# Outputs of the grouped attention kept in a tile on chip, and two sets of evacuations moved to the pool of eight small buffers

## The chip, the core and the metric

The kernel runs on one core of a Trainium2 chip. The metric is the device time of one execution in microseconds, as the median of several runs. Engines are named as the profile names them: PE is TensorE (PEld its weight loads), DVE is VectorE, ACT is ScalarE, POOL is GpSimd, SP is SyncE, which here only issues DMAs.

## What is computed

Two layers of an encoder trunk over 1024 tokens of width 1024 and a memory of 256 tokens. Each layer mixes tokens with four head groups side by side, attends to the memory, and ends in a gated ConvFFN. Cut to the part that the change touches:

```python
for l in range(DEPTH):                        # DEPTH = 2
    h = rms_norm(x, norm_mix[l])
    (ml_q, ml_k, ml_v, ml_o, ml_g, pool_u,
     d_q, d_k, d_v, g_q, g_k, g_v) = jnp.split(h @ w_in[l], splits, axis=-1)
    y_a = mlstm_mixer(ml_q, ml_k, ml_v, ml_o, ml_g, ...)       # 4 heads of 64, chunks of 64
    y_b = pool_mixer(pool_u, pool_w[l], pool_scale[l])
    y_c = diff_attention(d_q, d_k, d_v, ...)                   # 4 heads, two softmaxes each
    y_d = gqa_axial(g_q, g_k, g_v, ...)                        # 4 query heads, 2 key heads
    x = x + jnp.concatenate([y_a, y_b, y_c, y_d], axis=-1) @ w_out[l]
    x = x + cross_attention(rms_norm(x, norm_cross[l]), rms_norm(mem, norm_mem[l]), ...)
    x = x + conv_ffn(rms_norm(x, norm_ffn[l]), ...)
```

Inside the cross attention, the keys and values of the memory are `kv = memn @ w_ckv`, and the keys are normed per head.

## The kernel before

Activations lie transposed, features on the partitions: eight tiles of 128 features by 1024 tokens. Every factor of a product is split into a high and a low part (`hi`, `lo`), and a product is three matmuls (L353 hi·hi, L355 lo·hi, L357 hi·lo) that add up in one PSUM bank.

**Buffers.** All tiles come from pools with a fixed number of buffers; a tile that is asked for waits until the oldest holder of a buffer has been read for the last time, by a DMA too. `h` has 16 tiles of 128x1024, `t` 17 and `z` 4 of that size, `s` has eight tiles of 128x512, `e` two of 128x512. PSUM has two score tiles `sc`, three banks `tp` (of which one carries the attention's P·V sums) and one bank `fl` for filler work. `raw` and `wp` hold weights as they arrive and as they were split.

**Order.** A scheduler that models the engines puts the instructions of each engine in an order by priority. The steps of the attention (`attend`, L553) run under a raised priority. Between them the kernel pumps *filler*: generators in three queues that make a few matmuls at a time. Filler of queue 0 runs in the order in which it was filed: `memory_keys` (L1296), `memory_values` (L1367), the load and the split of the mixer's outputs (`mixed`, L1184, through `load_pair`, L1251), and the output projection (`residual_steps`, L1261).

**The mixer** (`mix`, L1069) of a layer first makes the projections. `ml_project` (L781) makes the mLSTM's query, key, value gate tiles; each of its two halves is scaled by DVE (L790) into an `e` tile and stored to DRAM (for the key `mkd`, L795). Then come the grouped attention and the differential attention. Both go in *passes*: one pass makes the scores of 128 queries against 1024 keys (L685, L688 grouped; L634 differential), DVE takes the row maximum (L479), ACT makes the exponentials (L482, an `h` tile). Then, four times 128x512, PE transposes probabilities (L537), ACT copies them as the high part into an `s` tile (L541), DVE makes the low part in another (L542), and PE makes the product with the values (L527, L528, L530). The grouped attention has 32 passes a layer, the differential one 64, whose two softmaxes POOL combines (L510, L511). For each pair of softmaxes DVE makes the factors of the combination (L508, L509).

**Outputs of the grouped attention.** `gqa_head` (L672) adds the two halves of a block of 64 features by 256 queries into half of an `s` tile and, for each second block, stores 64x512 to DRAM (`yd`). The filler `mixed` loads features 6 and 7 from there into a `z` tile and splits it into two `t` tiles (L1257, L1258). The other features of `yd` come from the mLSTM and from pooling.

**The memory's pairs.** `memory_keys` norms the keys and writes them as pairs in `e` tiles (L1361 ACT, L1362 DVE), stored to `ckd`. `memory_values` makes the products of the values, 24 matmuls a block (L1382 to L1384) in the `fl` bank, evacuates each as a pair into an `e` tile (L1388 ACT, L1389 DVE) and stores it to `cvd`.

**The output projection** is filler too: per 128 output features, four chunks of 18 matmuls (six feature tiles, three products each; 128x256) into halves of the `fl` bank, each evacuated by DVE onto the residual in a `z` tile (L1278). The last of eight feature tiles goes through a `tp` bank.

Of the kernel before, what the change touches and what calls it, by code (L numbers as in the profile page):

```python
# [23 lines left out]
HF = 512  # L24
# [27 lines left out]
class Net:  # L52
# [616 lines left out]
        )  # L669
        return q  # L670

    def gqa_head(self, l, h, kh, kl, V, q, ahead):  # L672
        nc = self.nc
        f, hh = divmod(h, 2)
        out = []

        def group(g):
            ws, tasks = [], {}
            for i in range(2):
                q0 = (g * 2 + i) * P  # L680

                def scores(sc, q0=q0):
                    for n in range(2):
                        sl = slice(n * HF, (n + 1) * HF)
                        nc.tensor.matmul(sc[:, sl], lhsT=q[:, q0 : q0 + P], rhs=kh[:, sl], start=True, stop=False)  # L685
                    for n in range(2):
                        sl = slice(n * HF, (n + 1) * HF)
                        nc.tensor.matmul(sc[:, sl], lhsT=q[:, q0 : q0 + P], rhs=kl[:, sl], start=False, stop=True)  # L688

                tasks[2 * i] = self.softmax(scores, ws)  # L690

            def evac(a, b):
                if g % 2 == 0:
                    out.append(self.s_())
                o = out[-1][:64]
                nc.vector.tensor_tensor(out=o[:, g % 2 * 256 : g % 2 * 256 + 256], in0=a, in1=b, op=ALU.add)
                if g % 2:
                    nc.sync.dma_start(
                        out=self.YD[6 + f, hh * 64 : hh * 64 + 64, g // 2 * HF : (g // 2 + 1) * HF], in_=o
                    )  # L700

            return tasks, self.mix_values(ws, V, evac)

        for g in range(4):
            if g == 2:
                ahead()
            yield group(g)
# [73 lines left out]
    def ml_project(self, l, j, H, dst, scale=None, sigmoid=False):  # L781
# [1 line left out]
        w = self.weights(self.d["w_fm"][l, j])  # L783

        def evac(sl, ps):
            t = self.e_()
            if scale is None:
                nc.vector.tensor_tensor(out=t, in0=ps, in1=self.RB[:, sl], op=ALU.mult)
            else:
                nc.vector.scalar_tensor_tensor(  # L790
                    out=t, in0=ps, scalar=scale, in1=self.RB[:, sl], op0=ALU.mult, op1=ALU.mult
                )
            if sigmoid:
                nc.scalar.activation(t, t, AF.Sigmoid)
            (nc.scalar if sigmoid else nc.sync).dma_start(out=dst[:, sl], in_=t)  # L795
# [273 lines left out]
    def mix(self, l, H, st):  # L1069
# [109 lines left out]
        self.flush(2)  # L1179
        self.fill(self.memory_keys(l, mem, self.h_, nc.gpsimd))  # L1180

        Y, Y2 = [], []

        def mixed(ks):  # L1184
            for k in ks:
                Y.append(self.load_pair(self.YD[k], self.tr_, nc.gpsimd if k < 7 else None))
                yield 0

        def heads():
            nonlocal nxt  # L1190
            for h in range(4):
                now = nxt

                def ahead():
# [4 lines left out]
                    else:  # L1199
                        nxt = self.diff_keys(l, 0, self.h_), self.diff_query(l, 0, 0, self.h_)  # L1200

                for g, (tasks, mix) in enumerate(self.gqa_head(l, h, *now, ahead)):
                    if (h, g) == (3,0):
                        self.flush(1)
                        self.fill(mixed((0, 1, 2, 3)))
# [45 lines left out]
    def load_pair(self, src, alloc, lo_engine=None, stage=False):  # L1251

        nc = self.nc
        x = self.tile(self.pw, [P, S], F32, "raw", bufs=4) if stage else self.z_()
        nc.sync.dma_start(out=x, in_=src)
        hi, lo = alloc(F32R), alloc(F32R)
        nc.scalar.copy(hi, x)  # L1257
        (lo_engine or nc.vector).tensor_tensor(out=lo, in0=x, in1=hi.bitcast(F32), op=ALU.subtract)  # L1258
# [37 lines left out]
    def memory_keys(self, l, mem, alloc, lo_engine):  # L1296
# [54 lines left out]
        for h in range(4):  # L1351
# [5 lines left out]
                    out=x0(h, f), in0=x0(h, f), scalar=self.col(l, C_CK + f), in1=pb, op0=ALU.mult, op1=ALU.mult  # L1357
                )
            for f in range(2):
                pr = self.e_(F32R).rearrange("p (s n) -> p s n", n=MEM)  # L1360
                nc.scalar.copy(pr[:, 0], x0(h, f))  # L1361
                nc.vector.tensor_tensor(out=pr[:, 1], in0=x0(h, f), in1=pr[:, 0].bitcast(F32), op=ALU.subtract)  # L1362
                nc.sync.dma_start(out=self.CK[h, :, f], in_=pr.bitcast(F32))
# [3 lines left out]
    def memory_values(self, l, mem, lo_engine):  # L1367
        nc, d = self.nc, self.d
        H, r = mem
        for h in range(4):  # L1370
# [6 lines left out]
            for t in range(2):  # L1377
# [6 lines left out]
                    nc.tensor.matmul(ps, lhsT=xl[:, tok], rhs=wh, start=False, stop=k == KT - 1)  # L1384
                    yield 3 * MEM / 2400
                rt = r[:, t : t + 1]
                pr = self.e_(F32R).rearrange("p (s n) -> p s n", n=MEM)
                nc.scalar.activation(pr[:, 0], ps, AF.Identity, bias=0.0, scale=rt)  # L1388
                nc.vector.scalar_tensor_tensor(  # L1389
                    out=pr[:, 1], in0=ps, scalar=rt, in1=pr[:, 0].bitcast(F32), op0=ALU.mult, op1=ALU.subtract  # L1390
# [580 lines left out]
```

## Time and profile before

| | us |
|---|---|
| Median of three runs | 3478.75 (3475.57 to 3484.61) |
| The profiled execution | 3481.47 |
| Its span in the trace | 3479.7 |
| Busy: PE, DVE, ACT, POOL | 3302.7, 2091.0, 1438.3, 570.1 |
| Layer 0: grouped attention, about | 388 to 551 |
| Layer 0: differential attention, about | 551 to 736 |
| Layer 0: its drain and the end of the output projection | 736 to 767 |
| Layer 1: grouped attention, about | 2104 to 2276 |

The span is the time between the first and the last instruction in the trace of one execution. Busy time of PE is that of matmuls; its weight loads run beside them. The stages are read from the first and the last score pass of each attention, and from the last matmul of the output projection.

### The profile page before, as it was taken

The page shows a single profiled execution, that of the slowest core. Times are in us where ns is not written, and L with a number is a line of the kernel's source. Part 1 is how long each engine was busy: PE and PEld are TensorE (multiplying, and loading weights), DVE is VectorE, ACT ScalarE, POOL GpSimd, SP SyncE. Part 2 cuts the span into 40 slices and gives each one's busy share as a digit, 9 for nine tenths or more (in the row PEclk, how much of TensorE's full clock was granted, in tenths as well). Part 3 has the DMA queues.
Part 4 walks back from the last instruction along what each step waited for, and adds up shares of the span by engine and source line. Part 5 has one row for each costly group of instructions (what it writes and reads, how often), then busy time and mean ns, then how long its engine had stood idle before and what let it go on. Part 6 is the DMA issues. An engine that isn't in the chain of part 4 may idle for free.

```text
span 3479.7 us, 43599 instructions
## 1 busy us (share of the span) xinstructions
PE 3302.7 (95%) x16782; PEld 2763.7 (79%) x16782; DVE 2091.0 (60%) x3308; ACT 1438.3 (41%) x2411; POOL 570.1 (16%) x442
## 2 busy tenths in 40 slices
PE   8999988999999999999999998889998999999999
PEld 8777877977777888778897777779787878788787
DVE  4444766874557777743535455778735577777432
ACT  4222556753444444321322245567525344334211
POOL 0110445730100000000002014367212000000000
PEclk9987899999999999999999888999999999999999
DMA  5343335322242222255533333344314312222654
GB/s 186 96 129 108 106 98 170 134 86 98 98 147 71 79 85 79 87 195 189 191 120 113 122 93 128 108 142 142 114 52 144 117 69 84 73 85 79 207 188 155
DMA packets 156195, 414.56 MB, mean 119 GB/s; under 512 B 31250, under 2 KB 49300, under 8 KB 155988
## 3 DMA queue, kind: packets, MB, share of 16 engines
q1 hardware_dynamic: 136372, 380.32, 32.8%
q10 hardware_dynamic: 19616, 31.46, 2.8%
q8 instruction: 132, 2.16, 0.3%
q14 instruction: 75, 0.61, 0.1%
HBM read 276.19 MB, written 128.19 MB: 116 GB/s over the span
## 4 chain that ended last, share of the span: by engine, by line
PE 79%; DVE 10%; DMA 6%; ACT 3%; issue 2%; POOL 1%; SPq 0%; ACTq 0%; DVEq 0%; POOLq 0%
PE sc L1701 15%; PE sc L353 12%; PE sc L355 11%; PE sc L357 11%; PE tp L1701 6%; PE tp L537 2%; DMA yd<-s 1%; DVE smax L479 1%; PE sc L634 1%; PE fl L353 1%; DMA raw<-w_ffn_in 1%; PE fl L355 1%; PE fl L357 1%; PE tp L528 1%; PE tp L1009 1%
## 5 line engine op out<-in xcount | busy, mean ns | idle before, releaser
L328 ACT CAST wp<-raw 128x1024 fp32r<-128x1024 f32 (+2 forms) x174 | 165.5, 952 | 577.5 <-PE sc L355 473.2
L353 PE MATMUL sc<-h,wp 128*128 128x512 f32 x1120 | 362.3, 404 | 16.4 <-DVE e L790 7.8
L357 PE MATMUL sc<-h,wp 128*128 128x512 f32 x1120 | 359.9, 401 | 5.0 <-DVE wp L329 5.0
L355 PE MATMUL sc<-h,wp 128*128 128x512 f32 x1120 | 362.0, 402 | 0.0
L1701 PE MATMUL sc<-h,wp 128*128 128x512 f32 x1320 | 336.7, 396 | 8.9 <-DVE t L1730 8.8
L1701 PE MATMUL sc<-t,wp 128*128 128x512 f32 x1320 | 327.9, 394 | 2.6 <-ACT t L1571 2.6
L1701 PEld LDWEIGHTS sc<-h,wp 128*128 128x128 f32 x1320 | 247.2, 190 | 71.5 <-DVE t L1730 19.7
L1701 PEld LDWEIGHTS sc<-t,wp 128*128 128x128 f32 x1320 | 251.3, 191 | 56.0 <-ACT t L1571 3.4
L353 PEld LDWEIGHTS sc<-h,wp 128*128 128x128 f32 x1120 | 212.7, 193 | 67.0 <-DVE e L790 8.2
L479 DVE TENSOR_REDUCE smax<-sc 128x1 f32<-128x1024 f32 x192 | 233.3, 1217 | 44.7 <-PE sc L688 22.6
L357 PEld LDWEIGHTS sc<-h,wp 128*128 128x128 f32 x1120 | 214.4, 193 | 56.1 <-DVE wp L329 8.7
L355 PEld LDWEIGHTS sc<-h,wp 128*128 128x128 f32 x1120 | 215.9, 193 | 48.9 <-issue 3.5
L482 ACT ACTIVATE h<-sc,smax 128x1024 f32<-128x1024 f32 x192 | 214.7, 1120 | 82.1 <-DVE smax L479 55.8
L1571 ACT CAST wp<-s 128x512 fp32r<-128x512 f32 x176 | 109.3, 623 | 312.4 <-PE sc L1701 302.2
L1290 DVE TENSOR_TENSOR z<-sc,z 128x1024 f32<-128x1024 f32 x64 | 78.3, 1224 | 260.3 <-PE sc L357 260.3
L542 DVE TENSOR_TENSOR s<-tp,s 128x512 fp32r<-128x512 f32 x256 | 172.8, 683 | 66.1 <-ACT s L541 64.9
L1701 PE MATMUL tp<-h,wp 128*128 128x512 f32 x792 | 203.0, 392 | 7.2 <-ACT wp L1571 7.2
L353 PE MATMUL sc<-t,wp 128*128 128x512 f32 x640 | 199.7, 394 | 7.4 <-ACT wp L328 4.6
L355 PE MATMUL sc<-t,wp 128*128 128x512 f32 x640 | 199.3, 393 | 2.7 <-DVE t L1258 2.7
L357 PE MATMUL sc<-t,wp 128*128 128x512 f32 x640 | 198.7, 391 | 0.0
L537 PE MATMUL tp<-identr,h 128*128 128x128 f32 x1024 | 181.9, 284 | 15.3 <-DVE s L542 11.7
L541 ACT CAST s<-tp 128x512 fp32r<-128x512 f32 x256 | 148.9, 587 | 109.2 <-PE tp L537 85.9
(428 smaller groups left out, 7043.0 us busy)
## 6 DMA issues: line engine op xcount, KB each, us to landing
raw<-w_ffn_in SPq DMA_DIRECT2D x88, 512.0 KB
xd<-z SPq DMA_DIRECT2D x72, 512.0 KB
z<-xd SPq DMA_DIRECT2D x72, 512.0 KB
gd<-t SPq DMA_DIRECT2D x44, 512.0 KB
z<-gd SPq DMA_DIRECT2D x44, 512.0 KB
raw<-w_ffn_out SPq DMA_DIRECT2D x32, 512.0 KB
raw<-w_fm SPq DMA_DIRECT2D x30, 512.0 KB
raw<-w_ck SPq DMA_DIRECT2D x16, 512.0 KB
```

What stands on the lines that cost most here:

```text
L328: nc.scalar.copy(hi, raw)
L353: nc.tensor.matmul(o, lhsT=hi[:, k, :], rhs=xh[:, f : f + m], start=first, stop=False)
L355: nc.tensor.matmul(o, lhsT=hi[:, k, :], rhs=xl[:, f : f + m], start=False, stop=False)
L357: nc.tensor.matmul(o, lhsT=lo[:, k, :], rhs=xh[:, f : f + m], start=False, stop=last)
L479: nc.vector.tensor_reduce(out=m, in_=sc, axis=AX.X, op=ALU.max, negate=True)
L482: nc.scalar.activation(e, sc, AF.Exp, bias=m, scale=1.0, accum_out=s)
L537: nc.tensor.transpose(tp[:, (2 * j + i) * P : (2 * j + i + 1) * P], w[:, (k + j) * P : (k + j + 1) * P], self.ident)
L541: nc.scalar.copy(eh, tp)
L542: nc.vector.tensor_tensor(out=el, in0=tp, in1=eh.bitcast(F32), op=ALU.subtract)
L1290: nc.vector.tensor_tensor(out=x, in0=ps, in1=x, op=ALU.add)
L1571: nc.scalar.copy(hi, x)
L1701: mm = lambda a, b, start, stop: nc.tensor.matmul(ps, lhsT=a, rhs=b, start=start, stop=stop, skip_group_check=not first)
```

## The change

The sums of the grouped attention's blocks are written straight into a tile of the `h` pool, `go`, two per layer (one for heads 0 and 1, one for heads 2 and 3; an odd head has partitions 64 to 127). The store and the load go, and `pair_of`, the second half of `load_pair`, splits `go` in place. `ml_project`, `memory_keys` and `memory_values` ask for `s` tiles instead of `e` tiles. Other users of `e` stay (among them `pool_steps` and `put_values`). The number of instructions on PE, DVE, ACT and POOL is the same; SP has 20 DMAs fewer.

```diff
@@ -669,10 +669,8 @@
         )
         return q
 
-    def gqa_head(self, l, h, kh, kl, V, q, ahead):
-        nc = self.nc
-        f, hh = divmod(h, 2)
-        out = []
+    def gqa_head(self, l, o, p0, kh, kl, V, q, ahead):
+        nc = self.nc
 
         def group(g):
             ws, tasks = [], {}
@@ -690,14 +688,7 @@
                 tasks[2 * i] = self.softmax(scores, ws)
 
             def evac(a, b):
-                if g % 2 == 0:
-                    out.append(self.s_())
-                o = out[-1][:64]
-                nc.vector.tensor_tensor(out=o[:, g % 2 * 256 : g % 2 * 256 + 256], in0=a, in1=b, op=ALU.add)
-                if g % 2:
-                    nc.sync.dma_start(
-                        out=self.YD[6 + f, hh * 64 : hh * 64 + 64, g // 2 * HF : (g // 2 + 1) * HF], in_=o
-                    )
+                nc.vector.tensor_tensor(out=o[p0 : p0 + 64, g * 256 : (g + 1) * 256], in0=a, in1=b, op=ALU.add)
 
             return tasks, self.mix_values(ws, V, evac)
 
@@ -783,7 +774,7 @@
         w = self.weights(self.d["w_fm"][l, j])
 
         def evac(sl, ps):
-            t = self.e_()
+            t = self.s_()
             if scale is None:
                 nc.vector.tensor_tensor(out=t, in0=ps, in1=self.RB[:, sl], op=ALU.mult)
             else:
@@ -1179,16 +1170,21 @@
         self.flush(2)
         self.fill(self.memory_keys(l, mem, self.h_, nc.gpsimd))
 
-        Y, Y2 = [], []
+        Y, Y2, go = [], [], []
 
         def mixed(ks):
             for k in ks:
-                Y.append(self.load_pair(self.YD[k], self.tr_, nc.gpsimd if k < 7 else None))
+                if k < 4:
+                    Y.append(self.load_pair(self.YD[k], self.tr_, nc.gpsimd))
+                else:
+                    Y.append(self.pair_of(go[k - 6], self.tr_, nc.gpsimd if k < 7 else None))
                 yield 0
 
         def heads():
             nonlocal nxt
             for h in range(4):
+                if h % 2 == 0:
+                    go.append(self.h_(F32))
                 now = nxt
 
                 def ahead():
@@ -1199,7 +1195,7 @@
                     else:
                         nxt = self.diff_keys(l, 0, self.h_), self.diff_query(l, 0, 0, self.h_)
 
-                for g, (tasks, mix) in enumerate(self.gqa_head(l, h, *now, ahead)):
+                for g, (tasks, mix) in enumerate(self.gqa_head(l, go[h // 2], 64 * (h % 2), *now, ahead)):
                     if (h, g) == (3,0):
                         self.flush(1)
                         self.fill(mixed((0, 1, 2, 3)))
@@ -1253,6 +1249,10 @@
         nc = self.nc
         x = self.tile(self.pw, [P, S], F32, "raw", bufs=4) if stage else self.z_()
         nc.sync.dma_start(out=x, in_=src)
+        return self.pair_of(x, alloc, lo_engine)
+
+    def pair_of(self, x, alloc, lo_engine=None):
+        nc = self.nc
         hi, lo = alloc(F32R), alloc(F32R)
         nc.scalar.copy(hi, x)
         (lo_engine or nc.vector).tensor_tensor(out=lo, in0=x, in1=hi.bitcast(F32), op=ALU.subtract)
@@ -1357,7 +1357,7 @@
                     out=x0(h, f), in0=x0(h, f), scalar=self.col(l, C_CK + f), in1=pb, op0=ALU.mult, op1=ALU.mult
                 )
             for f in range(2):
-                pr = self.e_(F32R).rearrange("p (s n) -> p s n", n=MEM)
+                pr = self.s_(F32R).rearrange("p (s n) -> p s n", n=MEM)
                 nc.scalar.copy(pr[:, 0], x0(h, f))
                 nc.vector.tensor_tensor(out=pr[:, 1], in0=x0(h, f), in1=pr[:, 0].bitcast(F32), op=ALU.subtract)
                 nc.sync.dma_start(out=self.CK[h, :, f], in_=pr.bitcast(F32))
@@ -1384,7 +1384,7 @@
                     nc.tensor.matmul(ps, lhsT=xl[:, tok], rhs=wh, start=False, stop=k == KT - 1)
                     yield 3 * MEM / 2400
                 rt = r[:, t : t + 1]
-                pr = self.e_(F32R).rearrange("p (s n) -> p s n", n=MEM)
+                pr = self.s_(F32R).rearrange("p (s n) -> p s n", n=MEM)
                 nc.scalar.activation(pr[:, 0], ps, AF.Identity, bias=0.0, scale=rt)
                 nc.vector.scalar_tensor_tensor(
                     out=pr[:, 1], in0=ps, scalar=rt, in1=pr[:, 0].bitcast(F32), op0=ALU.mult, op1=ALU.subtract
```

The scheduler puts the instructions in another order. On ACT, the first memory values (L1388) stand near the end of the grouped attention in layer 0; L482 is an exponential of the attention, L541 and L550 are evacuations of its transposes and of its sums. Before:

```order
L1361 CAST e_4934<-z_2848 128x256
L482 ACTIVATE h_4194,ssum_4172<-sc_4173,smax_4178 128x1024
L482 ACTIVATE h_4249,ssum_4228<-sc_4229,smax_4234 128x1024
L541 CAST s_4241<-tp_4236 128x512
L1388 ACTIVATE e_5128<-fl_4988,rtok_425_2833 128x256
L541 CAST s_4258<-tp_4253 128x512
```

And now:

```order
L541 CAST s_5067<-tp_5062 128x512
L541 CAST s_5094<-tp_5089 128x512
L1388 ACTIVATE s_5114<-fl_4974,rtok_426_2834 128x256
L482 ACTIVATE h_5076,ssum_1017_5055<-sc_5057,smax_5060 128x1024
L482 ACTIVATE h_5102,ssum_1017_5055<-sc_5084,smax_5087 128x1024
```

The first stood behind 30 of the layer's 96 exponentials and now stands behind 52, in the differential attention; the last of the eight stood behind 45 and now stands behind 85.

On PE, from the last score pass of layer 0's differential attention on; `tp<-identr` are transposes, `tp<-s` products with the values, `fl<-t,wp` the output projection, `sc<-h,wp` the next step of the layer. Before:

```order
L634 MATMUL sc_6582<-h_5746,h_6199 128x512 x2
L527 MATMUL tp_6509<-s_6533,h_5749 128x256
L537 MATMUL tp_6587<-identr,h_6392 128x128
L528 MATMUL tp_6509<-s_6534,h_5749 64x256
L537 MATMUL tp_6587<-identr,h_6449 128x128
L527 MATMUL tp_6509<-s_6533,h_5749 128x256
L537 MATMUL tp_6587<-identr,h_6392 128x128
L528 MATMUL tp_6509<-s_6534,h_5749 64x256
L527 MATMUL tp_6509<-s_6566,h_5749 128x256
L537 MATMUL tp_6587<-identr,h_6449 128x128
L353 MATMUL sc_7383<-h_6345,wp_7378 128x512 x2
```

And now:

```order
L634 MATMUL sc_6564<-h_5732,h_6181 128x512 x2
L537 MATMUL tp_6543<-identr,h_6205 128x128
L528 MATMUL tp_6491<-s_6488,h_5735 64x256
L537 MATMUL tp_6543<-identr,h_6264 128x128
L527 MATMUL tp_6491<-s_6487,h_5735 128x256
L537 MATMUL tp_6543<-identr,h_6205 128x128
L528 MATMUL tp_6491<-s_6488,h_5735 64x256
L537 MATMUL tp_6543<-identr,h_6264 128x128
L353 MATMUL fl_6169<-t_6139,wp_6619 128x256
L355 MATMUL fl_6169<-t_6140,wp_6619 128x256
L357 MATMUL fl_6169<-t_6139,wp_6620 128x256
```

Before, all but the last feature tile of the output projection was behind PE when the last pass began; now 378 of its matmuls follow that pass. In layer 1 the same places read alike.

## Rows read from the trace of the kernel before

**Rows 1.** The page: the span, and busy time by engine (share, instructions).
```profile
span 3479.7 us, 43599 instructions
...
PE 3302.7 (95%) x16782; PEld 2763.7 (79%) x16782; DVE 2091.0 (60%) x3308; ACT 1438.3 (41%) x2411; POOL 570.1 (16%) x442
```
**Rows 2.** Windows: start:end, length, busy us (instructions) by engine; granted clock, DMA share, GB/s.
```profile
core 0: us, PE busy (x) PEld busy (x) DVE busy (x) ACT busy (x) POOL busy (x), PEclk, DMA share, GB/s
388.00:551.00 163.00, 136.82 (x882) 118.32 (x880) 106.56 (x215) 91.55 (x176) 64.95 (x45) 0.93 0.35 111
551.00:601.00 50.00, 44.53 (x326) 41.23 (x326) 33.27 (x54) 35.58 (x63) 36.13 (x26) 0.97 0.53 181
601.00:736.00 135.00, 132.53 (x1017) 124.93 (x1016) 122.60 (x207) 98.03 (x174) 104.90 (x83) 1.00 0.33 115
736.00:750.00 14.00, 10.90 (x76) 8.91 (x75) 9.77 (x18) 8.23 (x15) 6.86 (x5) 1.00 0.07 22
...
2104.00:2276.00 172.00, 146.01 (x911) 126.23 (x912) 112.88 (x228) 95.95 (x186) 72.36 (x49) 0.91 0.34 109
```
**Rows 3.** Waits by line, 388 to 551, then 2104 to 2276: total us, times, longest.
```profile
ACT s L541 <- DMA yd<-s: 10.6, 1, 10.6
ACT e L1361 <- DMA ckd<-e: 9.5, 4, 5.6
...
ACT s L541 <- DMA yd<-s: 9.6, 1, 9.6
```
**Rows 4.** Grouped attention: chain (start, us, what), timeline (start, us, idle before), window.
```profile
428.81 18.63 DMA yd<-s
...
525.67 7.92 DMA ckd<-e
...
447.52 0.59 ACT L541 CAST s<-tp 128x512 fp32r<-128x512 f32 x1 [10.61 <-DMA yd<-s]
...
448.88 0.58 PE L527 MATMUL tp<-s,t 128*128 128x256 f32 x1 [8.04 <-DVE s L542]
...
449.00:453.00 4.00, 4.00 (x21) 4.00 (x22) 1.52 (x3) 3.35 (x8) 2.87 (x2) 0.57 0.12 51
```
**Rows 5.** The mLSTM's key projection: chain, timeline and window of layer 0; timeline of layer 1.
```profile
210.95 13.21 DMA mkd<-e
...
224.26 0.69 DVE L790 SCALAR_TENSOR_TENSOR e<-sc,rb 128x512 f32<-128x512 f32 x1 [11.04 <-DMA mkd<-e]
...
225.00 1.22 PE L353 MATMUL sc<-h,wp 128*128 128x512 f32 x2 [4.87 <-DVE e L790]
...
220.10:225.00 4.90, 0.04 (x1) 0.00 (x0) 0.74 (x2) 0.00 (x0) 0.00 (x0) 0.50 0.25 96
...
1944.19 1.22 PE L353 MATMUL sc<-h,wp 128*128 128x512 f32 x2 [2.96 <-DVE e L790]
...
1957.55 0.94 PE L947 MATMUL tp<-identr,t 64*128 64x64 f32 x8 [2.04 <-DMA t<-mkd]
```
**Rows 6.** Timeline of PE: a filler chunk, and two chunks in one bank at the end.
```profile
717.41 0.36 PE L353 MATMUL fl<-t,wp 128*128 128x256 f32 x1
...
719.53 0.28 PE L357 MATMUL fl<-t,wp 128*128 128x256 f32 x1
...
756.92 0.36 PE L353 MATMUL tp<-t,wp 128*128 128x256 f32 x1
...
759.83 0.39 PE L353 MATMUL tp<-t,wp 128*128 128x256 f32 x1 [0.52 <-DVE z L1278]
```
**Rows 7.** Groups of DVE by line and shape, 601 to 736: busy us, mean ns, idle before.
```profile
L479 DVE TENSOR_REDUCE smax<-sc 128x1 f32<-128x1024 f32 x50 | 60.8, 1218 | 7.5 <-PE sc L634 7.1
L542 DVE TENSOR_TENSOR s<-tp,s 128x512 fp32r<-128x512 f32 x48 | 32.2, 682 | 0.8 <-ACT s L541 0.5
...
L509 DVE SCALAR_TENSOR_TENSOR sfac<-ssum,nlam,sinv 128x1 f32<-128x1 f32 x25 | 9.0, 358 | 1.0 <-DVE rp L220 0.4
L643 DVE TENSOR_TENSOR h<-tp,s 64x256 f32<-64x256 f32 x12 | 4.9, 410 | 0.2
L508 DVE RECIPROCAL sinv<-ssum 128x1 f32<-128x1 f32 x25 | 3.9, 155 | 2.2 <-ACT h L482 2.1
```

## The prediction

> **What bounds the kernel now.** I read the engine shares first, then the stages of the mixer, then single waits. TensorE's matmuls fill 95% of the span of 3479.7 us; its weight loads run beside them, and no other engine is above 60% [rows 1]. The number and size of TensorE's instructions stay as they are, so the time can only change through TensorE's idle time and its clock. The profiled execution took 3481.47 us, the median of the three runs is 3478.75: I sum against the first and take 2.7 off at the end.
>
> The change touches one mixer stage per layer, in layer 0 from about 200 to 767 us. The windows [rows 2] show where TensorE idles there: 163 − 136.8 = 26.2 us in the stretch of the grouped attention (388 to 551), 50 − 44.5 = 5.5 and 135 − 132.5 = 2.5 in that of the differential attention (551 to 736), and 14 − 10.9 = 3.1 in the drain behind it (736 to 750). The differential attention is nearly gapless because the products of the memory values and the output projection lie between its passes; the grouped one is not, though its DVE, ACT and POOL are busy for 107, 92 and 65 of 163 us: it waits on latencies. Layer 1 looks alike (172 − 146.0 = 26 us of idle in 2104 to 2276).
>
> **Part 1: outputs of the grouped attention on chip.** It removes 16 stores and 4 loads of SP, and of its queue nothing else moves but the order. A stored output lies in an `s` buffer, which the next user gets only when the store has landed. Once a layer that is dear: one store takes 18.63 us on the chain, ACT's L541 waits 10.61 us for its buffer, and TensorE's next P·V product stands for 8.04 us [rows 3, 4]; behind it the granted clock of 449 to 453 us is 0.57, which costs another 4 × 0.43 = 1.7 us. Both go: −9.7 us. Layer 1 has the same wait with 9.6 us [rows 3]. The new evacuation writes the same 64x256 block on the same engine, so it costs nothing; a later load of the output for the pair disappears too, but the gap that follows it lies in the 5.5 us above and is counted there. The price is two `h` tiles, held until the heads are split.
>
> **Part 2: the shared pool.** *Projections.* The second half of the mLSTM's key product waits on DVE 11.04 us until a store of the first has left its `e` buffer (13.21 us on the chain), and TensorE stands for 4.87 us [rows 5]. With eight buffers this goes: −5 (0 if the load behind it then ends last, −8 if the granted clock of 0.50 in that window also rises some 5 us earlier, which is worth about 3). Layer 1 has two gaps of 2.96 and 2.04 us there [rows 5], so −5 too. *Memory keys.* ACT waits 9.5 us, four times, for key pairs in the two `e` buffers [rows 3]. In the new order the key evacuations lie 13 exps later and their buffers come back 34 to 82 instructions later instead of 15 to 43. I take two thirds of 9.5 as felt by TensorE: −6.3. With part 1 the grouped stage thus gains 9.7 + 6.3 = 16 us; bounds are 8 (the one gap alone) and 26 (all its idle time).
>
> *Memory values and the output projection: this is the dear part.* The pairs used to have the `e` pool almost to themselves. Now they ask for an `s` buffer, and the attention, with its higher priority, takes each one that comes free. The order of ACT shows it: the eight evacuations of the values (L1388) stood behind 30 to 45 of the layer's 96 exps, and now stand behind 52 to 85. The `fl` bank is not free before that, and the output projection comes after the values in the same queue. On TensorE all 192 products of the values were done by pass 13 of the 64 passes of the differential attention; now 24 until pass 21 and all at pass 46. The output projection has 504 matmuls in chunks of 18; they began at pass 14 and were done with the last pass. Now they begin at pass 53: 126 are done by the last pass, 90 in the drain, 234 in one unbroken run and 54 among the last 72. So 378 of them leave the stretch that they used to fill.
>
> *What the attention does without filler.* Its work per pass, from 50 passes in 601 to 736: on TensorE 132.5 us less 504 × 0.12 (start to start in a chunk, [rows 6]) = 72, so 1.44 us a pass. On DVE L479, L542, L509, L643 and L508 are 60.8 + 32.2 + 9.0 + 4.9 + 3.9 = 110.8, so 2.2 us a pass [rows 7]; with all that DVE did there it was 122.6 [rows 2], 2.45 a pass; the measured pass is 135/50 = 2.7. Without filler DVE sets the pass. No row shows a bare pass, so I bound it by 2.2 (DVE without a gap) and 2.7 (the pass does not get shorter, being held by latencies, as in the grouped stage, where DVE is busy for only 107 of 163 us), and take 2.45: DVE still has evacuations of values and statistics to do. TensorE's idle time is then, per layer:
> passes 0 to 21, no filler: 22 × (2.45 − 1.44) = 22;
> passes 22 to 46, with 168 products at 0.12 = 20.2: 25 × 1.01 − 20.2 = 5, taken as 7, as chunks don't fit each gap;
> passes 47 to 53: 7 × 1.01 = 7; passes 54 to 63: 10 × 1.01 = 10 is filled by 126 × 0.12 = 15, say 1.
> That is 37 where there were 8.0: +29. With 2.2 it is 17 + 1 + 5 + 0 = 23, so +15; with 2.7 it is 28 + 11 + 9 + 1 = 49, so +41.
>
> *The tail.* The 378 matmuls run behind the last pass. Two chunks in one bank don't overlap with the evacuation: the second started 2.91 us after the first, where 18 × 0.12 = 2.16 is work [rows 6]: 0.7 us each. The unbroken run has 13 chunks, so 12 × 0.7 = +8.4. The five chunks in the drain fill idle time of 3.1 us there: −3. Sum +5.
>
> **The sum.** Per layer +29 + 5 − 16 − 5 = +13; both layers +26. 3481.5 + 26 = 3507.5, less 2.7: **3505 us**.
>
> **Rivals.** *Faster.* The bare pass takes 2.2 us and the grouped stage loses all its idle time: +15 + 5 − 26 − 8 = −14 a layer, 3479 − 28 = 3451. For it: nearly all long waits named in that stage are those that the change removes. Against it: DVE without a gap over 64 passes is seen nowhere; in 601 to 736 it was busy for 91% with TensorE full. The Trainium skill (Perfetto Trace Analysis, Optimization Strategy) says that a repeated bubble on the engine that should be full can mean too few buffers, which is this rival's reading: more buffers, no bubbles. The ACT waits agree for two `e` buffers; the order shows that the eight are shared with a hungrier user.
> *Even.* A bare pass of 2.2 us with the central gains: +15 + 5 − 16 − 5 = −1 a layer, 3477.
> *Longer passes.* 2.7 us a pass: +41 + 5 − 16 − 5 = +25 a layer, 3529. For it: `h` is near full (13 to 16 of its 16 tiles taken up to pass 55 in the new order, where 10 to 12 were before from pass 16), so a score pass can wait for a probability tile; the memory tiles stay held until the last product of the values.
> *The waits come back in the `s` pool.* Key pairs now hold `s` buffers until their stores land, and an ACT evacuation of the attention waits behind one. The four waits of 9.5 us return, two thirds felt: the 6.3 us are not gained, +13 in all, 3518. It decides where a buffer is asked for again within the 8 us that a key store lasted on the chain [rows 4].
> *Clock.* In the bare passes TensorE works 1.44 of 2.45 us, 59%. Behind the gap of 8.04 us the clock fell to 0.57 [rows 4], and it was 1.00 at 98% busy [rows 2]. If passes 0 to 21 run at the lower level of 1.2 GHz, a pass needs 2.88 us of TensorE: +0.43 × 22 = 9.5 a layer, 3524. The Trainium skill (TensorE: Matmul & The Clock Gate, Part 4: PE-mode transpose) says that transposes do not count as work for the clock in the same way, which would favour this case, since each pass has four transposes. No stretch here shows transposes without other matmuls. The sum keeps the full clock.
>
> **Chances.** Forecast 0.43, faster 0.20, even 0.12, longer passes 0.10, waits come back 0.08, clock 0.07. About 0.3% (10 us) is what a measurement of this kernel can tell from no change: slower 0.65, within 0.15, faster 0.20. For the range I leave out the outer half of the faster rival, and above, the chance that the longer passes and another of the slow cases fall together: 3462 to 3542.
>
> **What would show it.** Right: the rows of the 8.04, 4.87 and `ckd` gaps are gone, 388 to about 551 is some 16 us shorter; the 64 passes of the differential attention take about 22 × 2.45 + 25 × 2.45 + 17 × 2.7 = 161 us instead of 185, with 37 us idle and DVE as releaser; then some 45 us more of `fl` matmuls behind the last pass, with a gap of about 0.5 us at each chunk. Wrong: passes near 2.2 us, or a TensorE that is idle in the grouped stage as before, with ACT waiting for DMA of an `s` buffer; or a second-layer result that differs from the first.

## The result, and the profile after

The changed kernel takes 3659.37 us (median of four runs, 3654.38 to 3659.91) beside 3479.61 of the kernel before (four runs): a ratio of 1.0521 [1.0499, 1.0543]. It is slower by 5.2%, as forecast in sign, but by 180 us instead of 26, and outside the range.

The page of the changed kernel, the lines that answer to [rows 1]:

```profile
span 3658.1 us, 43556 instructions
...
PE 3387.2 (93%) x16782; PEld 2804.7 (77%) x16782; DVE 2108.1 (58%) x3308; ACT 1436.8 (39%) x2411; POOL 572.7 (16%) x442
```

The span grew by 178.4 us. TensorE has the same 16782 matmuls and is busy for 84.5 us more; its idle time (span less busy) went from 177.0 to 270.9, by 93.9. So about half of the loss is idle time, and the other half is the same matmuls taking longer, most of it by a lower clock.

Where it lies: the start of the first score pass of each attention, of the last score matmul of the differential one and of the first matmul of the ConvFFN cut the span into stages. The first score pass of the grouped attention lies at 350.7 us in the kernel before, and at 2070.9 in layer 1, not at 388 and 2104 as in the table of the kernel before; in layer 0 TensorE is busy for 36.9 of the 37 us in between, so the idle time read there stays. Length in us, and TensorE's idle time in brackets:

| stage | layer 0 before | after | layer 1 before | after |
|---|---|---|---|---|
| grouped attention | 200.5 (26) | 202.7 (22) | 204.6 (26) | 197.4 (20) |
| differential attention | 184.7 (8) | 222.9 (48) | 186.1 (10) | 223.6 (48) |
| last pass to ConvFFN | 323.9 (22) | 375.1 (26) | 324.8 (21) | 374.7 (26) |

Up to the first grouped pass it is 350.7 and 352.1; the rest between the layers 1011.2 and 1016.1. So all of it arises in the differential attention (+38 a layer) and behind it (+51).

Windows of the changed kernel (columns as in [rows 2]): the grouped and the differential attention of layer 0 and what follows up to the end of the output projection; then the differential one cut where passes 0, 21, 46, 53 and 63 start, so passes 0 to 20, 21 to 45, the last part of these by itself, 46 to 52 and 53 to 62.

```profile
core 0: us, PE busy (x) PEld busy (x) DVE busy (x) ACT busy (x) POOL busy (x), PEclk, DMA share, GB/s
352.00:555.00 203.00, 181.41 (x1057) 154.68 (x1056) 131.38 (x259) 111.42 (x212) 80.92 (x61) 0.87 0.31 97
554.80:777.70 222.90, 174.80 (x949) 140.75 (x949) 159.32 (x249) 130.97 (x237) 132.69 (x103) 0.82 0.25 78
777.70:857.70 80.00, 73.22 (x571) 68.73 (x569) 27.98 (x61) 16.49 (x28) 16.33 (x10) 1.00 0.32 112
...
555.00:616.00 61.00, 45.98 (x218) 33.66 (x218) 53.16 (x79) 42.03 (x80) 36.25 (x31) 0.82 0.26 87
616.00:730.00 114.00, 85.98 (x475) 70.95 (x474) 64.60 (x110) 58.45 (x104) 61.47 (x45) 0.81 0.25 77
696.00:730.00 34.00, 26.17 (x128) 21.70 (x126) 15.29 (x32) 11.60 (x24) 7.45 (x7) 0.65 0.14 46
730.00:744.00 14.00, 9.71 (x29) 5.81 (x28) 12.32 (x15) 9.25 (x17) 13.46 (x11) 0.62 0.26 85
744.00:777.00 33.00, 32.22 (x225) 29.48 (x225) 28.40 (x45) 20.73 (x38) 21.31 (x17) 0.90 0.20 69
```

In the kernel before the two windows of the differential attention had clocks of 0.97 and 1.00 [rows 2]; here it is 0.82 over the stage. By that, as an estimate, 174.8 × 0.18 = 31 us of the stage went to the clock, where it had been 2. The sum of the stage is then: +40 of idle time (48 instead of 8), +29 of clock, −45 for the 378 matmuls that moved behind the last pass, +2 for 16 products of the values that moved in: +26 of 38 measured. The other 12 us are busy time that was not traced further. One candidate is matmuls in short groups: one that stands alone is busy for 0.28 us, and takes 0.12 from start to start in a chunk [rows 6].

Passes 0 to 20 take 61/21 = 2.9 us each, and DVE is busy for 53 of 61, so it is nearly full. Passes 21 to 45 take 114/25 = 4.6 us, and no engine is full there: DVE has 65 of 114, POOL 61, ACT 58. What they wait for, in the waits of the whole stage (columns as in [rows 3]):

```profile
POOL h L510 <- DVE sfac L509: 33.0, 15, 11.3
DVE s L542 <- ACT s L541: 29.0, 13, 7.3
...
ACT s L541 <- PE tp L537: 21.1, 15, 5.9
...
PE sc L634 <- ACT h L482: 17.2, 21, 1.9
...
ACT h L482 <- PE tp L276: 6.8, 1, 6.8
```

Each engine waits for the one ahead of it in the pass: a chain. And TensorE lengthens that chain with the filler itself. In the timeline (start, us) the products of the values start 0.21 us apart instead of 0.12, in a stretch with a granted clock of 0.65 (696 to 730), and the transposes stand behind a block of them, for which ACT waits 5.88 us (last line). Further on, the 16 small products that norm the attention's outputs take 3.57 us while ACT waits 6.8 us behind them:

```profile
699.12 0.58 PE L1382 MATMUL fl<-wp,h 128*128 128x256 f32 x1 [0.29 <-DVE s L1389]
699.50 0.41 PE L1383 MATMUL fl<-wp,h 128*128 128x256 f32 x1
699.71 0.41 PE L1384 MATMUL fl<-wp,h 128*128 128x256 f32 x1
...
703.22 0.60 PE L537 MATMUL tp<-identr,h 128*128 128x128 f32 x4
...
711.78 3.57 PE L276 MATMUL tp<-cons,h 128*128 128x2 f32 x16
...
703.85 0.59 ACT L541 CAST s<-tp 128x512 fp32r<-128x512 f32 x1 [5.88 <-PE tp L537]
```

### The profile page after: what moved, and what is told of

It is laid out like the page before. It is cut to its first block, busy times and chain, and to the rows that moved or that the text cites. A ratio compares the mean times of both kernels' runs of the same rounds, so it can differ in the third digit from the quotient of the medians.

```text
span 3658.1 us, 43556 instructions
## 1 busy us (share of the span) xinstructions
PE 3387.2 (93%) x16782; PEld 2804.7 (77%) x16782; DVE 2108.1 (58%) x3308; ACT 1436.8 (39%) x2411; POOL 572.7 (16%) x442
## 5 line engine op out<-in xcount | busy, mean ns | idle before, releaser
L482 ACT ACTIVATE h<-sc,smax 128x1024 f32<-128x1024 f32 x192 | 214.3, 1118 | 138.3 <-DVE smax L479 66.7
L542 DVE TENSOR_TENSOR s<-tp,s 128x512 fp32r<-128x512 f32 x256 | 174.4, 685 | 109.3 <-ACT s L541 107.0
L537 PE MATMUL tp<-identr,h 128*128 128x128 f32 x1024 | 200.1, 308 | 37.0 <-POOL h L511 24.4
L1701 PE MATMUL tp<-h,wp 128*128 128x512 f32 x792 | 202.7, 391 | 8.4 <-ACT wp L1571 8.4
L541 ACT CAST s<-tp 128x512 fp32r<-128x512 f32 x256 | 148.8, 587 | 135.5 <-PE tp L537 120.1
L357 PE MATMUL sc<-t,wp 128*128 128x512 f32 x640 | 198.9, 392 | 0.0
```

The costliest lines, as they stand in the source:

```text
L357: nc.tensor.matmul(o, lhsT=lo[:, k, :], rhs=xh[:, f : f + m], start=False, stop=last)
L482: nc.scalar.activation(e, sc, AF.Exp, bias=m, scale=1.0, accum_out=s)
L537: nc.tensor.transpose(tp[:, (2 * j + i) * P : (2 * j + i + 1) * P], w[:, (k + j) * P : (k + j + 1) * P], self.ident)
L541: nc.scalar.copy(eh, tp)
L542: nc.vector.tensor_tensor(out=el, in0=tp, in1=eh.bitcast(F32), op=ALU.subtract)
L1701: mm = lambda a, b, start, stop: nc.tensor.matmul(ps, lhsT=a, rhs=b, start=start, stop=stop, skip_group_check=not first)
```

## The experiments: which part does it

Theory A: the memory values' pairs in `s` tiles hold the output projection back, as filler comes late. Rival B: the two `h` tiles of the on-chip outputs starve the attention. Each ratio below is against runs of the kernel before on the same chip, with its 95% interval.

**Only the outputs on chip** (the changed kernel with all three pools put back):

```diff
-            t = self.s_()
+            t = self.e_()
...
-                pr = self.s_(F32R).rearrange("p (s n) -> p s n", n=MEM)
+                pr = self.e_(F32R).rearrange("p (s n) -> p s n", n=MEM)
```

> Only the outputs of the grouped attention stay on chip; all evacuations keep their two e buffers. Theory A (late filler): the loss of 180 us comes from the memory values in the s pool, whose ring of eight buffers ties them to the attention; here the output projection is again done with the last pass of the differential attention, so the time is 3460 to 3485, less by the yd waits (8 to 10 us a layer) if nothing takes their place. Rival B (full h pool): two more h tiles held starve the score passes: 3520 or more, with idle TensorE before score passes and exponentials waiting for an h tile.

Measured: 3491.79 us, 1.006 [1.004, 1.008]. That is 7 us over theory A's number and far under rival B's, so rival B falls as the cause of the large loss: the differential stages take 186.6 and 189.6 us. But the part gains nothing and costs 0.6%; the grouped stages take 208.7 and 209.5.

**Only the mLSTM projections in `s`** (the kernel before with the first of these edits reversed):

> Kernel before with only the mLSTM projections in s tiles. The forecast gave it -5 us a layer: 3469. What the changed kernel's trace shows speaks against it: TensorE stands 12.7 and 14.7 us for the load of mkd, so the wait only moves to that load: 3475 to 3485, with one gap of about 12 us instead of 4.9 plus 1.4.

Measured: 3481.76 us, 1.0021 [1.0002, 1.004]. No gain, as expected from the second reading.

**Only the memory's pairs in `s`** (the kernel before, keys and values changed as in the diff of the change):

> Kernel before with only the memory pairs (keys and values) in s tiles. Theory A: the whole loss is here, 3640 to 3680, with granted clock near 0.82 and some 40 to 50 us of idle in each layer's differential attention. Rival B (the h tiles, or several causes that add up): under 3560.

Measured: 3635.8 us, 1.0476 [1.0444, 1.0509]. Nearly the whole loss, 4 us under theory A's number. The differential stages take 222.7 and 223.6 us, with 52 and 49 of idle; the first of them, and the grouped stage ahead of it:

```profile
345.00:534.00 189.00, 169.32 (x1033) 144.85 (x1032) 126.94 (x255) 108.98 (x205) 81.43 (x62) 0.91 0.33 106
533.90:756.60 222.70, 170.32 (x971) 136.31 (x970) 158.97 (x252) 132.48 (x240) 131.34 (x102) 0.85 0.27 87
```

**Everything but the values** (the changed kernel, L1387):

```diff
-                pr = self.s_(F32R).rearrange("p (s n) -> p s n", n=MEM)
+                pr = self.e_(F32R).rearrange("p (s n) -> p s n", n=MEM)
                 nc.scalar.activation(pr[:, 0], ps, AF.Identity, bias=0.0, scale=rt)
```

> Changed kernel with the memory values' pairs back in e tiles; keys, mLSTM projections and the on-chip outputs stay as changed. Theory A: the values alone hold the output projection back, since they come before it in the filler queue and share its PSUM bank: 3455 to 3480, output projection done with the last pass. If the keys in s tiles take part in the loss: 3520 or more.

Measured: 3483.97 us, 1.0033 [1.0016, 1.005]. One word, in the values alone, takes 1.0521 to 1.0033, 4 us over theory A's number. The differential stage is 182.9 us at a clock of 0.99:

```profile
350.00:554.70 204.70, 184.26 (x1093) 158.01 (x1092) 133.05 (x262) 113.93 (x214) 85.11 (x63) 0.87 0.32 101
554.70:737.60 182.90, 171.66 (x1274) 158.07 (x1273) 165.63 (x263) 129.73 (x235) 135.40 (x105) 0.99 0.41 134
```

Theory A stands: the values' pairs are the cause of the loss. The values alone in `s` were not run; it follows from this run and from the keys alone, which cost 0.3% (below). The remaining +0.3% is clear of the interval, but small.

## The experiments: why the values come late

The prediction said that the attention outranks the values and takes each buffer. A sharper reading: a pool hands its buffers out in turn, in the order in which the program is written. A pair of the values in `s` gets the buffer of the attention's tile that was written eight `s` tiles earlier, and can't be evacuated before that tile is done, however early its products could run. In the `e` pool the filler ran ahead of the place where it is written; in `s` it can't. The kernel pumps 0.2 us of filler per slot (one step of the attention) of the grouped attention and 0.6 in the differential one; written earlier, the same pairs in the same pool should come earlier. All three runs are the changed kernel with other rates:

```diff
-                    yield 0.2, tasks, mix
+                    yield 0.6, tasks, mix
...
-                    yield 0.6, tasks, mix
+                    yield 1.2, tasks, mix
```

> Changed kernel, all of it, but the filler is written into the program earlier: the kernel pumps 0.6 us of filler per slot of the grouped attention instead of 0.2, and 1.2 instead of 0.6 in the differential one. Theory A in its sharper form (the ring of s buffers ties an evacuation to the place where it is written, eight s tiles behind the attention's, and the filler was written too late): the products of the values are through by pass 10 and the output projection by pass 58, so the loss goes: 3440 to 3490. Rival B (the attention outranks the pairs and takes every buffer, wherever they are written): the order on the chip may change but the passes still wait for s tiles: 3560 or more.

Measured: 3536.63 us, 1.02 [1.0168, 1.0232]. Neither number. The differential attention is better than before (175.7 and 174.4 us, and 325.8 and 325.5 behind it): there the theory holds, with every pair in `s`. But the grouped attention grows to 234.5 and 229.0 us, with 40 us of idle, and a clock of 0.84:

```profile
352.00:586.50 234.50, 194.68 (x1176) 168.60 (x1175) 137.01 (x273) 121.54 (x230) 92.02 (x67) 0.84 0.34 111
586.50:762.20 175.70, 164.72 (x1208) 151.47 (x1206) 159.36 (x254) 124.81 (x224) 128.95 (x102) 0.97 0.33 109
```

```profile
ACT t L1257 <- DMA z<-yd: 19.9, 3, 15.3
```

```profile
467.16 1.19 PE L683 MATMUL sc<-h,h 128*128 128x512 f32 x2 [11.80 <-DMA h<-gqd]
```

The last two, from the waits and the timeline, are waits of that stage: of ACT for the outputs of other heads to come back, and of TensorE before a score pass for a query that is loaded from DRAM (`gqd`). The stage holds 120 more products of the values than in the changed kernel, 14 us of work, and is 32 us longer; the rest is idle time, 40 us instead of 22 and 20. Where that comes from was not taken apart; the two waits are the candidates. These stages are read from an execution of 3523.84 us, the fastest of the four.

**The first rate alone** (0.6 in both):

> As the run before, with 0.6 us per slot in both attentions: the values start in the grouped attention, where TensorE idled 20 to 22 us, and the output projection is spread to pass 58 as there. Theory A: 3440 to 3490, within 15 us of the run before. Rival B: 3560 or more.

Measured: 3543.11 us, 1.02 [1.018, 1.0219]. Neither number again, but within 15 us of the run before: the same picture, 231.4 and 182.0 us in the two stages of layer 0.

**The second rate alone** (0.2 and 1.2), for a dose between:

> Changed kernel, with the filler written earlier in the differential attention alone (1.2 us per slot instead of 0.6; the grouped attention keeps 0.2). In the order the values are then through by pass 30 instead of 46, and 414 of the 504 matmuls of the output projection by the last pass instead of 126; passes 0 to 12 still have no filler. Theory A (the loss is the filler that comes late, in dose): 13 bare passes lose about 2.77 - 1.44 = 1.3 us each where 43 us were lost in the whole stage before it, and 5 chunks follow the last pass instead of 21: some 15 us a layer over the kernel before, ratio 1.007 to 1.014, with the grouped stage as in the changed kernel, 197 to 205 us. Rival B (s tiles are short wherever the pairs are written): the differential stage stays at 215 us or more, ratio 1.03 or more.

Measured: 3534.37 us, 1.018 [1.0155, 1.0204]: between the two numbers, nearer to theory A. The grouped stage is as expected (201.3 and 199.0 us). The differential one is 204.3 and 205.6, some 20 over before, with 24 of idle and a clock of 0.92, and 7 us more follow behind it:

```profile
555.00:759.30 204.30, 180.57 (x1237) 160.73 (x1237) 168.23 (x265) 134.52 (x241) 140.59 (x107) 0.92 0.36 118
```

With the filler after pass 13 in place the excess over the kernel before, in this stage and behind it, falls from 38 + 51 to 20 + 7 us a layer, and with the filler wholly in place (first run) to −9 + 2 in layer 0. The dose fits in order; its size was again estimated without the clock, which by the same estimate as above took 180.6 × 0.08 = 14 us.

## The experiments: the clock

If TensorE's idle time lowers the clock, and the clock lengthens the chain, then more work for TensorE should cost less than nothing. Each score matmul of the differential attention is made twice into the same place:

```diff
-                    for n in range(2):
-                        nc.tensor.matmul(
+                    for n in range(2):
+                        for _ in range(2):
+                            nc.tensor.matmul(
```

> Changed kernel; each score matmul of the differential attention is made twice into the same place, so 128 more matmuls of 512 columns a layer, about 31 us at the full clock and 62 at half. The filler stays where it was. Question: what part of the passes' length is the clock. If the low granted clock (0.82 in that stage) follows from TensorE's idle time, more work lifts it and the extra work is mostly given back: 3640 to 3690, clock 0.88 or more there. If the passes are bound by their chain of waits at whatever clock: 3700 to 3780, clock as before.

> Kernel before with the same score matmuls made twice. TensorE is full there, so the whole of it shows: 3530 to 3545, less the 8 us a layer that TensorE still idles. It is the price of the extra matmuls at the full clock.

Measured: the kernel before takes 3529.1 us, 1.0165 [1.014, 1.019], 56 us more, near the price at full clock. The changed kernel takes 3635.13 us, 1.0471 [1.045, 1.0491]: with 128 more matmuls in each layer it is *faster* than without them, 1.0471 against 1.0521, whose intervals don't touch (two and four executions). It lies 5 us under the first of the two numbers expected. Its two differential stages, and then layer 0's in the kernel before with the same doubling:

```profile
559.30:772.70 213.40, 183.42 (x1083) 152.87 (x1083) 157.50 (x251) 133.66 (x240) 134.35 (x106) 0.92 0.25 82
2356.20:2567.20 211.00, 179.23 (x1084) 148.07 (x1083) 155.36 (x251) 133.41 (x240) 134.50 (x106) 0.95 0.26 83
```

```profile
548.10:754.90 206.80, 202.86 (x1459) 187.59 (x1458) 159.90 (x261) 133.34 (x235) 142.47 (x108) 1.00 0.35 117
```

The clock rises from 0.82 to 0.92 and 0.95, and the stages shrink from 222.9 and 223.6 us to 213.4 and 211.0, although the same matmuls lengthen the stage of the kernel before from 184.7 to 206.8. TensorE is idle for 30 us instead of 48, which the added work alone would do too; that the stage gets shorter, it would not. So the clock was not only a price of the idle time: at the lower clock TensorE's own steps of a pass are longer, and the pass with them. The transposes of layer 0's stage (L537) are busy for 273 ns each in the kernel before, 318 in the changed one and 296 with the doubling. One thing besides the clock moved: a block of 24 products of the values lies behind the start of pass 22 instead of ahead of it. What that is worth was not run.

## The experiments: where the expected gain went

The forecast gave the other parts −21 us a layer, mostly in the grouped attention. With the values back in `e` the kernel should have been faster by that, and it isn't. In the changed kernel the 8.04 us before the P·V product [rows 4] are gone; TensorE instead stands here, before the first score pass of the third head (first line: changed kernel; second: only the outputs on chip):

```profile
461.86 1.19 PE L683 MATMUL sc<-h,h 128*128 128x512 f32 x2 [6.29 <-issue]
```

```profile
458.03 1.19 PE L683 MATMUL sc<-h,h 128*128 128x512 f32 x2 [9.31 <-issue]
```

That pass reads a query that is loaded into an `h` tile. It began at 457.19 us in the kernel before, without a wait, and at 461.86 and 458.03 here:

```profile
457.19 0.63 PE L685 MATMUL sc<-h,h 128*128 128x512 f32 x2
```

The load is issued at 432.19 us before and 438.28 after (434.48 with only the outputs on chip):

```profile
432.19 0.58 SPq L667 DMA_DIRECT2D h<-gqd  x1
```

```profile
438.28 1.02 SPq L667 DMA_DIRECT2D h<-gqd  x1
```

The trace names no releaser for the two gaps ("issue"). But in both kernels the pass begins 23.6 us behind the issue of the load, and 24.5 behind it in the run with both rates raised, where the trace names the load. By that, as an estimate, the load of the kernel before landed at about 455.8 us, 1.4 us before its pass: of the 8.04 us of the store's wait hardly more than that could be gained, as the load would then have ended last.

Theory: two `h` tiles for the outputs make it later still. Three runs: the keys alone in `s`, where the gain does not depend on that; the outputs alone, in tiles of the `t` pool; and both (with the projections in `s`), the best that the parts could give.

```diff
-                    go.append(self.h_(F32))
+                    go.append(self.t_(F32))
```

> Kernel before with only the memory keys' pairs in s tiles; values, projections and the stored outputs as before. In the run with both memory pairs in s tiles the grouped attention was 11 and 12 us shorter than before, with the same yd wait in it, so it is the ckd waits that went. Theory: that gain is the keys', and the values in e tiles keep the output projection on time: 10 to 22 us under the kernel before, ratio 0.994 to 0.997. Rival: the shorter grouped stage was only the values' work moved out of it (24 products fewer): ratio 0.999 to 1.002.

Measured: 3484.06 us, 1.0033 [1.002, 1.0047]. Both expectations missed: not faster, a little slower. The ckd waits are gone and the grouped stage is 197.5 and 200.5 us instead of 200.5 and 204.6, but the differential one is 187.4 and 194.2, with 16 and 15 us of idle instead of 8 and 10. Part of what the grouped stage gained has only moved. DVE's low parts of the eight key pairs (L1362) lie in the grouped stage of layer 0 in the kernel before (first two lines: its two stages; after the length, DVE's busy time on L1362), and in the differential one here:

```profile
351.00:551.00 200.00, 4.69 (x8) 0.91 0.35 112
551.20:735.90 184.70, 0.00 (x0) 0.99 0.38 133
```

```profile
346.30:543.80 197.50, 0.00 (x0) 0.91 0.35 111
543.80:731.20 187.40, 6.87 (x8) 0.98 0.42 135
```

It is so in both layers, and in each of the runs with the keys in `s` and the first rate at 0.2. So the keys' waits did not go because there are more buffers for them: like the values, the keys come later.

> Only the outputs of the grouped attention stay on chip, as in the run of that part alone (ratio 1.006), but in tiles of the t pool, not of h. Theory: there the yd wait went but TensorE then stood 9.3 us before the score pass whose query load had to wait for an h buffer; with go in t tiles the load is issued earlier and the part is worth what the forecast gave it: ratio 0.994 to 0.998. Rival: the load is late in any case and ends last behind the removed wait: ratio 1.000 to 1.006, with the same gap before L683.

Measured: 3470.4 us, 0.9992 [0.9974, 1.0009]. In tiles of `t` the part costs nothing (1.006 in `h`), so the `h` tiles were its price: the `h` tiles of rival B do cost something, 0.6%. The gap before L683 is down to 1.0 us, the load is issued at 420.41, and the grouped stages take 188.5 and 198.9 us, 12 and 6 less than before. Still the median is not lower by more than the interval: the differential stage of layer 0 takes 193.3, 8.6 more, that of layer 1 is 0.5 shorter. Here the two traced executions mislead when taken as a whole: 3464.28 beside 3481.47 us, 17 us apart where the medians are 4 apart.

> Changed kernel with the values' pairs back in e tiles and the on-chip outputs in t tiles. If both theories of the two runs above hold, this adds them up: ratio 0.988 to 0.995, faster than both kernels. If the query load is late anyway: 0.997 to 1.003.

Measured: 3486.9 us, 1.0036 [1.0022, 1.0049], slower than either number. The grouped stages are 194.3 and 192.4 us, 6 and 12 less than before, with 17 us of idle; the differential ones 193.1 and 191.5, 8 and 5 more, with 15 of idle, and 7 and 3 more behind them:

```profile
348.60:542.90 194.30, 177.11 (x1086) 151.62 (x1085) 130.75 (x259) 112.76 (x213) 85.70 (x63) 0.91 0.34 110
542.90:736.00 193.10, 178.53 (x1296) 165.91 (x1295) 165.64 (x268) 133.32 (x241) 135.83 (x105) 0.96 0.39 123
```

So the waits of the grouped stage can be taken away, and were, but the time comes back, most of it in the next stage: over the span TensorE's idle time (span less busy) is 182.8 us here and 177.0 before. Part of it is the keys, whose evacuations are in the differential stage here too (7.1 us of DVE). Why else the differential attention idles more when the grouped one ends earlier is not settled; no run took it apart. Each stage is read from one execution: the end of the kernel, from the first ConvFFN matmul of layer 1 on, whose text no run changes, takes 688 to 697 us in the fourteen traces, so differences of 2 or 3 us in a stage of 190 are no more than that. No version beat the kernel before by more than its interval.

## Why the prediction was wrong, point by point

The sum gave +13 us a layer; the traces show +89. Of the 76 us between them, 21 are the gains of the grouped stage and the projections that did not come, 1 lies behind the last pass, and 54 lie in the differential attention, which by the sum takes 185 + 29 − 45 = 169 us and took 223. (The 161 us given among the signs of being right are a second figure for the same stage, 8 us less.) So the step that failed is "What the attention does without filler": it sets the pass at 2.45 us, with 1.44 us of TensorE at the full clock. Measured are 2.9 us in the first 21 passes and 4.6 in the next 25, at a granted clock of 0.82 and 0.81, with 48 us of idle time instead of 37, and TensorE busy for 175 us where the sum leaves 132.

- **What bounds the kernel**: held, with one half of it not drawn out. "The time can only change through TensorE's idle time and its clock", and it did, by 94 and 84 us; the sum had no term for the clock.
- **Yd wait, −9.7**: the 8.04 us went, and a query load took their place (6.29 us in this kernel). The step that failed here is "Both go": it was not asked what was late next behind the store. Grouped stage: +2 in layer 0 and −7 in layer 1, forecast −16.
- **Projections, −5**: nothing (1.0021 for that part alone). The bound "0 if the load behind it then ends last" was the right value: TensorE now waits for the load in one piece.

```profile
233.99 1.09 PE L938 MATMUL tp<-identr,t 64*128 64x64 f32 x8 [12.72 <-DMA t<-mkd]
```

- **Values and output projection**: the mechanism was right, and the run with one word undone shows it. The reason for it was not: by the runs with other rates it is the buffers' turn, not the priority.
- **Bare passes, +29**: the mis-sized term. Idle time is 48 us in the stage instead of 37; by the four stretches 15, 28, 4 and 1 us where the sum has 22, 7, 7 and 1. Passes 0 to 20 take 2.9 us instead of 2.45, above the upper bound of 2.7, and passes 21 to 45 take 4.6: there the filler that should have filled the gaps left 28 us of them. The timeline shows blocks of it ahead of transposes that ACT waits for; that these blocks make the most of the 28 us is argued and was not run. In passes 46 to 52, 2.0 us were seen.
- **The clock**: listed as a rival with 0.07 and 9.5 us a layer, for passes 0 to 21 alone. By the estimate above it was 31 us a layer, over all passes, and the doubling shows that the lower clock lengthens the passes too: the two were treated as separate cases, and came together. The row for it stood in the prediction: 0.57 behind a single gap of 8 us. The rule of the Trainium skill (TensorE: Matmul & The Clock Gate, Part 4: PE-mode transpose) that was cited beside it points the same way, though the runs don't show whether transposes count less: in the doubling, score matmuls were added, not exchanged for transposes.
- **The tail, +5 beside the 45 us of moved matmuls**: right. 80 us from the last pass to the end of the projection instead of 31; 12 waits of about 0.5 us for a bank, 6.5 us where the sum had 8.4 (one of them in the timeline, and the group of these matmuls, behind the last pass):

```profile
801.06 0.39 PE L353 MATMUL fl<-t,wp 128*128 128x256 f32 x1 [0.52 <-DVE z L1278]
```

```profile
L353 PE MATMUL fl<-t,wp 128*128 128x256 f32 x126 | 37.2, 295 | 6.5 <-DVE z L1278 6.5
```

- **Memory keys, −6.3, and the waits that come back in the `s` pool**: no wait for a `ckd` store is left in the grouped stage of the changed kernel, but not because it has buffers to spare. The key evacuations, which the prediction saw 13 exps later, have left the stage: DVE's eight lie 27 to 48 us behind the start of the differential attention, where they lay 7 to 32 us ahead of it. The gain was booked without their cost there.

Per layer: grouped stage and projections, forecast −21, measured about 0; differential stage, forecast −16, measured +38; behind it, forecast +50, measured +51.

## What to carry to other kernels

A pool's buffers come round in the order of the program: to let background work use the buffers of urgent work ties the two together, and a small private pool can be worth more than a large shared one. On an engine that is full, filler that comes late is to be priced as idle time and as the lower clock that follows it together, not as two cases. And when a wait is removed, name the next load behind it before the gain is booked, and look whether the work that waited has only gone to the next stage.

## What the runs showed of the hardware

A stage in which TensorE idles can get shorter when TensorE gets more to do: 128 more 512-column matmuls a layer took the granted clock of a stage in which it idled for 48 of 223 us from 0.82 to 0.92 and 0.95, and the stage from 223 to 213 and 211 us. The sum of the idle time alone does not give the clock: the grouped stage idled for 26 of 200 us at 0.91 in the kernel before (line below), and for 22 of 203 at 0.87 in the changed one.

```profile
351.00:551.00 200.00, 173.71 (x1048) 147.71 (x1047) 132.93 (x269) 113.77 (x216) 81.70 (x63) 0.91 0.35 112
```
